# Three attention-gate column blocks computed in layer 0's first, k-outer GEMM

## The chip, the core and the metric

The kernel runs on one core of one Trainium2 chip. Engines are TensorE (PE, matmuls, with its weight loads PEld), VectorE (DVE), ScalarE (ACT), GpSimd (POOL) and SyncE (SP), which issues most DMA transfers. The metric is device time in microseconds of one execution, the median over runs.

## The reference

One inference step of a two-layer hybrid backbone on 512 latent and 128 context tokens (T = 640 columns in all), width 2048, float32. Cut to what matters:

```
mod = silu(cond) @ w_ada + b_ada                 # adaLN: shift, scale, gate (3 x 2048)
h   = rmsnorm(x) * (1 + scale) + shift
q, k, v, ag, lx, lg, hv, hx1, hx0, hg = split(h @ w_in)      # 7168 columns
att = rmsnorm(diff_attention(q, k, v)) * silu(ag)            # 8 heads, 1024 columns
lru = rglru(dwconv(lx)) * silu(lg)                           # 512 columns
hy  = hx0 * long_conv(hx1 * hv) * silu(hg)                   # 512 columns
x   = x + gate * (concat(att, lru, hy) @ w_out)
```

The column block of `ag` that belongs to head h only enters the last product of `att`, after the attention of that head.

## The kernel before

Activations lie transposed: 16 chunks of 128 features by 640 tokens. Each float32 product is made of three matmuls on split operands (wh with A high, wh with A low, wl with A high), each over two halves of 320 columns, so one 128-column block of a projection is 16 chunks times six matmuls. A weight load (`load_w`, line 369) brings up to four chunks of one block by a DMA on SP's queue into one of four `wr` buffers; ACT casts it to wh and DVE subtracts wl (lines 178, 179). The usual `gemm` (line 403) runs one column block over all 16 chunks in PSUM.

Layer 0 begins differently, because its adaLN vectors need 33 MB of w_ada before all of h exists. `run` (from line 1200) goes through five groups of chunks, (0,2), (2,2), (4,4), (8,4), (12,4). In each group it passes over the list `first`, eight column blocks (hx0 and hg, four each), with `gemm_part` (line 512): PSUM holds the sum over the group's chunks, and ACT (first group) or DVE (the others, line 527) adds it to a tile in SBUF, one of the `early` tiles. Between the blocks stand steps of `ada_piece` (line 299), each one transfer of 512 KB of w_ada and its matmuls (line 313). Two chains of steps, scale and shift, belong to each group; in all there are 10, 20, 38, 56 and 74 steps up to the end of groups 0 to 4, of which 14 come before the first block. After block number NAT (4, counted from 0) the steps that the next group needs are completed and its normalisation (`norm`) begins, one chunk after each following block, the rest behind the last block. A chunk is transposed on PE (lines 1231, 1237), scaled on DVE (line 509), cast on ACT and split on DVE.

Then `hyena_gates(0)` turns the early tiles into gates in DRAM (`md`). `layer` runs four RG-LRU blocks, the attention of eight heads, the first NAG = 3 attention gates (`gate`, line 1004, through the pool `agq`), the Hyena projections `hyena_u` with the filters, and then the Hyena convolutions beside the other five gates. A gate is a projection, a silu (`silu2`), a load of the head's attention output from `md` and of its normaliser from `rd`, two DVE products (lines 1012, 1013) and a store to `md`.

Work is ordered by a list scheduler at build time: program order is the priority, an instruction whose inputs aren't ready is passed over for a later one, weight loads are preferred, and every engine and queue then runs its own list strictly in order. So projections fill PE's gaps beside the softmax of a head.

The other adaLN pieces (layer 0's gate, layer 1's shift and scale: 12 pieces of 16 steps, 192 steps) are computed on DVE by `ada_steps` (line 320; lines 333, 335), called as a hook in `gemm` at a rate per weight load: 1 in the RG-LRU stage, 0.5 in attention, 0.75 for the first gates and the Hyena projections, 1 for the other gates and the output projection. What is left is drained near the end of `out_proj(0)`, ahead of the normalisation for layer 1.

Of the kernel before, what the change touches and what calls it, by code (L numbers as in the profile page):

```python
# [22 lines left out]
T = NL + NP  # L23
# [6 lines left out]
COL_Q, COL_K, COL_V, COL_AG = 0, 1024, 2048, 3072  # L30
COL_LX, COL_LG = 4096, 4608
COL_HV, COL_HX1, COL_HX0, COL_HG = 5120, 5632, 6144, 6656
# [4 lines left out]
WR = 4  # L37
CVB = 3
LEAD = 4
NAT = 4  # L40
MIX_ORDER = [*range(8, 12), *range(4), *range(12, 16), *range(4, 8)]


# [86 lines left out]
NAG = 3  # L130
# [7 lines left out]
class K:  # L138
# [865 lines left out]
    def gate(self, l, hs, m0, c, pool, store, bufs=1):  # L1004

        nc, V = self.nc, self.nc.vector
        sg = self.silu2(self.proj(l, m0, hs), pool, bufs=1)
        m = self.tl(pool, [128, T], tag="gm", bufs=bufs)
        nc.sync.dma_start(m, self.md[l][c])
        R = self.tl(pool, [128, T], tag="R")  # L1010
        nc.sync.dma_start(R, self.rd[l][c:c + 1, :].to_broadcast([128, T]))
        V.tensor_tensor(m, m, R, op=ALU.mult)
        V.scalar_tensor_tensor(m, m, self.par[l]["sg"], sg, op0=ALU.mult, op1=ALU.mult)
        if store or self.taps:
            nc.sync.dma_start(self.md[l][c], m)
        return m
# [183 lines left out]
    def run(self):  # L1200
        nc, tc, V = self.nc, self.tc, self.nc.vector
        dt = lambda shape, name: tc.dram_tile(shape, F32, name=name)
        self.xd = [dt([KC, 128, T], f"xd{l}") for l in range(DEPTH)]
        self.md = [dt([KC, 128, T], f"md{l}") for l in range(DEPTH)]
        self.gd = [dt([2, 5, 128, 2, 256], f"gd{l}") for l in range(DEPTH)]
        self.g1 = [dt([2, 3, 256], f"g1{l}") for l in range(DEPTH)]
        self.hd = [dt([128, 384], f"hd{l}") for l in range(DEPTH)]
        self.rd = [dt([NH, T], f"rd{l}") for l in range(DEPTH)]
        self.early = {}
        sm = self.sm  # L1210
        first = [c + j * 128 for j in range(4) for c in (COL_HX0, COL_HG)]
        w = self.i["w_in"][0]
        with ExitStack() as st, self.tc.tile_pool(name="ps0", bufs=1, space=PSUM) as self.pst:
            self.A1 = self.ctx.enter_context(self.pool("A1", 24))
# [11 lines left out]
            hs = []  # L1226
# [22 lines left out]
            def ada_to(n):  # L1249
                nonlocal done  # L1250
                while done < n:
                    next(adas, None)
                    done += 1
# [7 lines left out]
            for gi, (k0, kn) in enumerate(groups):  # L1261
                more = gi + 1 < len(groups)
                nxt = iter(())
                for n, m0 in enumerate(first):
                    self.gemm_part(self.load_w(w, k0, m0, kn), m0, hs, k0, kn, self.early[0, m0])
                    ada_to(done + (2 if kn == 4 or gi else 1))
                    next(nxt, None)
                    if more and n == NAT:
                        ada_to(steps[gi + 1])
# [9 lines left out]
                self.par.append(self.params(1, nc.sync))  # L1279
            self.sm = sm  # L1280
            self.hyena_gates(0, hs)
        self.pss = self.ctx.enter_context(self.ppool("pss", 1))
        self.pst = self.ctx.enter_context(self.ppool("pst", 2))
        self.hook = self.ada_steps([(0, p) for p in range(8, 12)] + [(1, p) for p in range(8)])
        self.layer(0, hs)
        hs = self.out_proj(0)
# [262 lines left out]
```

## Time and profile before

| what | value |
|---|---|
| median of three runs | 2725.28 us (2720.43 to 2726.11) |
| the profiled execution | 2730.49 us, of which 2728.5 us are its span |
| mean granted TensorE clock | 0.987 |
| PE busy | 2599.8 us (95%) |
| DVE busy | 1920.0 us (70%) |
| ACT, POOL busy | 1076.9 us (39%), 261.6 us (10%) |
| DMA, mean over the span | 130 GB/s |

Busy time of PE is the union of its matmuls, which overlap: a matmul of 320 columns is shown with 0.31 us, and the next one starts about 0.147 us later. The bracket behind an instruction in a timeline is the idle time of its engine before it and what ended that.

### The profile page before, as it was taken

To read this page: it belongs to the slowest core of one execution; us is meant where nothing else is said; L and a number is where in the kernel's file an instruction comes from. 1 tells how busy PE (TensorE), PEld (TensorE's weight loads), DVE (VectorE), ACT (ScalarE), POOL (GpSimd) and SP (SyncE) were. 2 spreads that over 40 slices of the span, in tenths; PEclk is the share of its full clock that TensorE was granted. 3 is DMA by queue.
4 is the path that set the end of the run, shared out by engine and by line. 5 is a ranking of instruction groups with operands and counts; after the bars stand their busy time and mean duration, and the time that the engine had idled before them with its cause. 6 is when DMAs were issued, how large, how long until landed. Compare 5 with 4: busy or idle time off the path is not lost. (4 is left out here: it accounts for less than half of the span.)

```text
span 2728.5 us, 45802 instructions
## 1 busy us (share of the span) xinstructions
PE 2599.8 (95%) x17503; PEld 2485.5 (91%) x17503; DVE 1920.0 (70%) x3499; ACT 1076.9 (39%) x1970; POOL 261.6 (10%) x352
## 2 busy tenths in 40 slices
PE   4999989999999999989998999999999999999998
PEld 2589989999999998889998999999999999989997
DVE  3568997787888787777679467877777756564333
ACT  4224545455554222132235256444455522223222
POOL 1000220000000221200001012000000021120000
PEclk9999999999999999999999999999999999999999
DMA  8773443332333545576664323422322252345333
GB/s 256 247 239 118 128 136 90 90 106 66 102 93 114 173 136 158 158 227 200 191 196 147 117 69 86 127 87 86 101 75 64 59 166 79 106 143 158 98 94 118
DMA packets 439911, 354.83 MB, mean 130 GB/s; under 512 B 26746, under 2 KB 367618, under 8 KB 439436
## 3 DMA queue, kind: packets, MB, share of 16 engines
q1 hardware_dynamic: 428618, 336.39, 41.1%
q10 hardware_dynamic: 9586, 9.42, 1.1%
q0 software_dynamic: 1488, 6.10, 0.6%
q8 instruction: 137, 2.24, 0.3%
q14 instruction: 82, 0.67, 0.1%
HBM read 316.51 MB, written 35.32 MB: 129 GB/s over the span
## 5 line engine op out<-in xcount | busy, mean ns | idle before, releaser
L420 PE MATMUL g<-A,wh 128*128 128x320 f32 x8320 | 1614.1, 311 | 5.6 <-ACT A L178 5.0
L420 PEld LDWEIGHTS g<-A,wh 128*128 128x128 f32 x8320 | 1321.3, 189 | 7.3 <-ACT A L178 5.3
L420 PE MATMUL g<-A,wl 128*128 128x320 f32 x4160 | 963.9, 310 | 0.0
L178 ACT CAST wh<-wr 128x512 fp32r<-128x512 f32 (+1 forms) x592 | 362.1, 613 | 966.3 <-PE g L420 696.2
L420 PEld LDWEIGHTS g<-A,wl 128*128 128x128 f32 x4160 | 702.6, 189 | 0.2
L179 DVE TENSOR_TENSOR wl<-wr,wh 128x512 fp32r<-128x512 f32 (+1 forms) x592 | 429.2, 728 | 339.0 <-ACT wh L178 323.9
L335 DVE SCALAR_TENSOR_TENSOR adas<-wa,cs,adas 128x512 f32<-128x512 f32 x480 | 363.9, 784 | 61.4 <-DMA wa<-in_w_ada 60.1
L1160 ACT ACTIVATE e<-e,mx 128x768 f32<-128x768 f32 (+1 forms) x160 | 133.7, 835 | 69.2 <-DVE e L1159 68.9
L1159 DVE TENSOR_SCALAR_CACHE_REDUCE e<-pS 128x768 f32<-128x768 f32 (+1 forms) x160 | 131.0, 819 | 9.1 <-PE pS L713 3.9
L1122 POOL TENSOR_TENSOR oq<-ot 128x640 f32<-128x640 f32 x16 | 20.9, 1309 | 912.5 <-ACT ot L1118 689.7
L713 PE MATMUL pS<-kk,qq 128*128 128x384 f32 (+1 forms) x288 | 100.3, 348 | 3.9 <-DVE e L1159 3.4
L521 PE MATMUL gp<-A,wh 128*128 128x320 f32 x512 | 101.9, 318 | 1.0 <-ACT wh L178 1.0
L397 PE MATMUL g<-A,wh 128*128 128x320 f32 (+2 forms) x384 | 92.9, 324 | 8.9 <-DVE A L492 5.9
L521 PEld LDWEIGHTS gp<-A,wh 128*128 128x128 f32 x512 | 79.7, 189 | 23.0 <-issue 11.2
L713 PE MATMUL pS<-kl,qq 128*128 128x384 f32 (+1 forms) x288 | 95.2, 331 | 0.0
L179 DVE TENSOR_TENSOR wtl<-pt,wth 128x512 fp32r<-128x512 f32 (+1 forms) x144 | 70.1, 522 | 29.6 <-ACT wth L178 29.3
L178 ACT CAST wth<-pt 128x512 fp32r<-128x512 f32 (+1 forms) x144 | 59.7, 459 | 61.6 <-PE pt L1103 60.0
L313 PE MATMUL pa<-wada,csw 128*32 128x512 f32 (+1 forms) x320 | 52.7, 565 | 28.9 <-DVE st L436 21.5
L397 PEld LDWEIGHTS g<-A,wh 128*128 128x128 f32 x384 | 67.0, 194 | 14.4 <-DVE A L492 8.3
L1396 DVE SCALAR_TENSOR_TENSOR xf<-g,mod,xo 128x128 f32<-128x128 f32 (+3 forms) x96 | 38.3, 432 | 55.8 <-PE g L420 23.2
L1166 DVE SCALAR_TENSOR_TENSOR e<-e,rz,e 128x768 f32<-128x768 f32 (+1 forms) x80 | 70.6, 882 | 1.7
L713 PEld LDWEIGHTS pS<-kk,qq 128*128 128x128 f32 x288 | 54.0, 187 | 14.7 <-DVE e L1159 8.8
(353 smaller groups left out, 3159.7 us busy)
## 6 DMA issues: line engine op xcount, KB each, us to landing
wr<-in_w_in SPq DMA_DIRECT2D x440, 256.0 KB
wa<-in_w_ada SPq DMA_DIRECT2D x256, 256.0 KB
wada<-in_w_ada SPq DMA_DIRECT2D x64, 512.0 KB
wr<-in_w_out SPq DMA_DIRECT2D x128, 256.0 KB
mx<-md SPq DMA_DIRECT2D x28, 320.0 KB
md<-ot SPq DMA_DIRECT2D x16, 320.0 KB
gm<-md SPq DMA_DIRECT2D x16, 320.0 KB
R<-rd SPq DMA_DIRECT2D x16, 320.0 KB
```

The source lines that it names most:

```text
L178: self.nc.scalar.copy(hi, src)
L179: self.nc.vector.tensor_tensor(lo, src, hi.bitcast(F32), op=ALU.subtract)
L313: nc.tensor.matmul(acc[32 * q:32 * q + 32, :], lhsT=self.csw[:, k, :], rhs=w[:, j, :], start=k < 4, stop=k >= 12, tile_position=(0, 32 * q))
L335: nc.vector.scalar_tensor_tensor(acc[:, s], w, c, acc[:, s], op0=ALU.mult, op1=ALU.add)
L397: nc.tensor.matmul(p[:, j, o:o + c1 - c0], lhsT=w[:, c, :], rhs=rhs[k][x][:, c0:c1], start=(a == 0 and c == 0 and n == 0), stop=(a == 3 an ...
L420: nc.tensor.matmul(p[:, j, :HT], lhsT=w[:, c, :], rhs=rhs[k][x][:, j * HT:(j + 1) * HT], start=(a == 0 and c == 0 and n == 0), stop=(a == ...
L521: nc.tensor.matmul(p[:, j, :HT], lhsT=w[:, c, :], rhs=rhs[k0 + c][x][:, j * HT:(j + 1) * HT], start=(c == 0 and t == 0), stop=(c == n - 1 ...
L713: self.nc.tensor.matmul(out, lhsT=a, rhs=b, start=(n == 0), stop=(n == len(pairs) - 1))
L1159: V.tensor_scalar(e[:, :nk].rearrange("p (a b) -> p a b", a=nhf), ps[:, :nhf, :hw], -1.0, None, op0=ALU.mult, op1=ALU.min, accum_out=mx)
L1160: nc.scalar.activation(e[:, :nk], e[:, :nk], AF.Exp, scale=-1.0, bias=mx, accum_out=Z[:, c:c + 1])
L1166: V.scalar_tensor_tensor(es[0][:, :nk], es[1][:, :nk], rz[:, 1:2], es[0][:, :nk], op0=ALU.mult, op1=ALU.add)
L1396: V.scalar_tensor_tensor(x[:, a:b], p, mod[:, 32 + m, s:s + 1], xo[:, a:b], op0=ALU.mult, op1=ALU.add)
```

## The change

Three more column blocks, the attention gates of heads 0 to 2, join the list `first`, so each of the five groups passes over 11 blocks, and there are 11 early tiles. After `hyena_gates(0)` their silu is taken and stored to a new DRAM tensor `agd`. In layer 0, `gate` loads this for heads 0 to 2 in place of its own projection and silu; with that the hook is not called there. NAT goes from 4 to 8. Layer 1 is as before.

```diff
-NAT = 4
+NAT = 8
@@ gate
-        sg = self.silu2(self.proj(l, m0, hs), pool, bufs=1)
+        if l == 0 and c < NAG:
+            sg = self.tl(pool, [128, T], tag="th")
+            nc.sync.dma_start(sg, self.agd[c])
+        else:
+            sg = self.silu2(self.proj(l, m0, hs), pool, bufs=1)
@@ run
+        self.agd = dt([NAG, 128, T], "agd")
-        first = [c + j * 128 for j in range(4) for c in (COL_HX0, COL_HG)]
+        first = [c + j * 128 for j in range(4) for c in (COL_HX0, COL_HG)] + [COL_AG + h * 128 for h in range(NAG)]
@@ run, behind the first GEMM
             self.hyena_gates(0, hs)
+            with self.pool("ag0") as ap:
+                for h in range(NAG):
+                    th = self.silu2(self.proj(0, COL_AG + h * 128, hs), ap)
+                    nc.sync.dma_start(self.agd[h], th)
```

## Rows read from the trace of the kernel before

**Rows 1.** The page, parts 1 and 2: engines' busy time; DMA by 40 slices.
```profile
PE 2599.8 (95%) x17503; PEld 2485.5 (91%) x17503; DVE 1920.0 (70%) x3499; ACT 1076.9 (39%) x1970; POOL 261.6 (10%) x352
...
DMA  8773443332333545576664323422322252345333
```

**Rows 2.** Waits of PE over the span: total us, times, longest us.
```profile
PE pa L313 <- DVE st L436: 21.5, 1, 21.5
...
PE pa L313 <- DMA wada<-in_w_ada: 7.4, 5, 3.3
...
PE g L397 <- DVE A L492: 5.9, 9, 1.2
```

**Rows 3.** Stretches of the first GEMM: length, busy us, clock, DMA share, GB/s.
```profile
40.00:60.00 20.00, 17.71 (x131) 10.79 (x127) 9.93 (x45) 6.77 (x16) 0.00 (x0) 0.83 0.94 289
...
140.00:160.00 20.00, 20.00 (x136) 14.31 (x135) 11.45 (x21) 5.63 (x9) 0.00 (x0) 1.00 0.98 311
...
50.00:120.00 70.00, 65.93 (x395) 40.31 (x395) 38.41 (x89) 22.55 (x44) 1.50 (x9) 0.98 0.82 250
```

**Rows 4.** PE's timeline around its wait for w_ada: start, us, instruction, idle before.
```profile
87.00 1.06 PE L313 MATMUL pa<-wada,csw 128*32 128x512 f32 x8
...
95.36 1.58 PE L313 MATMUL pa<-wada,csw 128*32 128x512 f32 x4 [3.26 <-DMA wada<-in_w_ada]
96.87 1.43 PE L521 MATMUL gp<-A,wh 128*128 128x320 f32 x4
98.23 1.50 PE L313 MATMUL pa<-wada,csw 128*32 128x512 f32 x4
99.66 0.56 PE L521 MATMUL gp<-A,wl 128*128 128x320 f32 x2
```

**Rows 5.** PE's timeline in the last group of the first GEMM.
```profile
201.08 1.35 PE L521 MATMUL gp<-A,wh 128*128 128x320 f32 x7
...
207.56 0.75 PE L521 MATMUL gp<-A,wh 128*128 128x320 f32 x4
208.14 0.45 PE L521 MATMUL gp<-A,wl 128*128 128x320 f32 x2
208.44 0.75 PE L521 MATMUL gp<-A,wh 128*128 128x320 f32 x4
```

**Rows 6.** DVE's groups from 180 to 230 us: busy us, mean ns, idle before.
```profile
L527 DVE TENSOR_TENSOR e<-e,gp 128x640 f32<-128x640 f32 x13 | 10.7, 819 | 3.1 <-PE gp L521 2.9
L179 DVE TENSOR_TENSOR wl<-wr,wh 128x512 fp32r<-128x512 f32 x13 | 8.9, 685 | 0.0
...
L509 DVE TENSOR_SCALAR hn<-pn,mod 128x512 f32<-128x512 f32 x4 | 3.2, 802 | 0.0
```

**Rows 7.** Stretches around attention's end, the first gates and the Hyena projections.
```profile
843.00:868.00 25.00, 25.00 (x175) 24.78 (x174) 24.36 (x51) 14.87 (x31) 0.00 (x0) 1.00 0.36 108
868.00:905.00 37.00, 35.27 (x231) 33.99 (x231) 32.11 (x50) 14.33 (x28) 6.38 (x10) 0.95 0.51 157
```

**Rows 8.** Timelines of DVE, POOL and PE around attention's end.
```profile
872.22 0.88 DVE L1013 SCALAR_TENSOR_TENSOR gm<-gm,sg,th 128x640 f32<-128x640 f32 x1
...
898.20 0.82 DVE L439 TENSOR_TENSOR oh<-oh,ol 128x640 f32<-128x640 f32 x1
...
893.18 0.16 POOL L746 MEMSET cv<- 128x1 f32 x3
...
883.29 0.56 PE L713 MATMUL pt<-ol,onesr 128*128 128x320 f32 x2 [1.73 <-POOL ol L1124]
```

**Rows 9.** The stretch of the RG-LRU stage's later part.
```profile
300.00:420.00 120.00, 104.58 (x665) 102.55 (x664) 113.59 (x163) 56.96 (x80) 26.68 (x21) 0.93 0.45 131
```

**Rows 10.** The hook's DVE operations from 843 us on; DVE and stretch at the layer border.
```profile
L335 DVE SCALAR_TENSOR_TENSOR adas<-wa,cs,adas 128x512 f32<-128x512 f32 x67 | 52.0, 799 | 6.2 <-DMA wa<-in_w_ada 6.0
...
1400.67 1.29 DVE L342 TENSOR_REDUCE mod<-pt 128x4 f32<-128x512 f32 x2 [2.90 <-PE pt L341]
...
1440.00:1460.00 20.00, 15.69 (x89) 12.89 (x88) 20.00 (x39) 14.53 (x33) 7.56 (x7) 1.00 0.54 162
```

## The prediction

> **What bounds the kernel now.** I read the busy shares first: TensorE (PE) is busy 95% of the span and no other engine comes near [rows 1]. Then I asked what PE waits for [rows 2]: the largest wait, 21.5 us, is before its first matmul and the change leaves it alone. What remains is scattered. So 42 us of PE work that only moves from one full stretch to another is worth nothing in itself; the change can win only idle time that the moved work fills, and lose only idle time that it makes. The reader should therefore look at the two places: where the work goes (the first GEMM, about 50 to 228 us) and where it leaves (the attention gates after layer 0's attention, about 843 to 905 us).
>
> **Where it goes.** The slices show the DMA engines 70 to 80% busy in the first 200 us [rows 1], which looks like a transfer-bound stage with room on PE. By stretches it is not so: from 50 to 120 us PE is busy 65.93 of 70 us [rows 3], and PE's only wait on a w_ada piece after the GEMM has begun is 3.26 us at 95.36 [rows 4]. Behind that stall the clock fell to its lower level (1.2 GHz): three bundles at 95.36, 96.87 and 98.23 stand 1.51, 1.36 and 1.43 us apart (to 99.66), where they take about 1.0, 0.7 and 1.0 at 2.4 GHz, so 1.6 us more. Stall and slow clock are 3.3 + 1.6 = 4.9 us: this is all the idle time that the moved work can fill here.
>
> **The moved work.** In the last k group, where no adaLN piece is in between, four wh and two wl matmuls (one k chunk of one column block) take 208.44 - 207.56 = 0.88 us [rows 5]. A block has 16 chunks: 14.1 us; three blocks: 42.2 us. They are added to the first GEMM and taken from the gates, with the same shapes. There PE is busy 25.00 of 25 us and 35.27 of 37 [rows 7], so the blocks fill their place after attention: minus 42.2 us there.
>
> **Is the stall gone?** By the code each group runs its blocks with adaLN steps between (512 KB of w_ada each, 0.524 MB). Before, groups 0 and 1 take 16 block loads of 0.131 MB and steps 14 to 44: 2.1 + 15.7 = 17.8 MB. Their PE work is 16 x 1.76 us, some 27 us of steps (1.06 us each from the four-chunk groups on [rows 4], half of it before) and about 8 us of transposes and filter matmuls: 64 us, so 280 GB/s are asked. After, 22 loads and steps 14 to 47 are 20.2 MB against 39 + 30 + 8 = 77 us: 262 GB/s. The queue delivered 289 in 40 to 60 us and 311 in 140 to 160, at a share of 0.98 [rows 3]. NAT = 8 also takes away the burst: before, five steps stand in a row behind the fifth block of group 1; after, two follow every block. I take the 4.9 us as won; the bounds are 0 and 4.9.
>
> The Trainium skill (DMA: Bandwidth & Descriptors, Specifications) gives a core about 358 GB/s from HBM; by that figure the stall would go with a wide margin, and the sum is the same. The 311 GB/s at a share of 0.98 say that here little more is to be had.
>
> **What is late next in the first GEMM.** With NAT = 8 of 11 blocks the next group's chunks come after blocks 9 and 10, so three of four chunk transposes stand behind the last block instead of two. Each needs two DVE operations (802 ns the larger [rows 6]), an ACT cast and a DVE subtraction before PE may read the chunk. Before, PE bridged this by interleaving two blocks (the bundle of seven wh matmuls at 201.08 [rows 5]) without a gap. One chunk more is at worst 1.7 us (two chunks of work, 1.76 us, against some 3.5 us) at each of four group borders: 0 to 6.8 us. Three of the borders have adaLN steps to fill with, so I take 1. DVE gets 12 additions of 0.82 us, 15 splits (nine of 0.69, six of half width, say 0.4), and three silu products of about 0.8: 21 us in a stretch that grows by 37 us; it isn't the bound. The three stores to agd are behind the hyena gates on SP and nothing on PE waits for them.
>
> **Where it leaves.** Gates 0 to 2 become three loads, two DVE products (0.88 us the second [rows 8]) and a store each. Their inputs exist long before attention ends, so they lie beside it; in SP's queue the loads stand ahead of weight loads, but four weight buffers are 4 x 3.5 = 14 us ahead. What now fills PE's gaps beside head 7's softmax is no longer an attention gate but the first Hyena projections. Their eviction needs three `cv` buffers in memory that attention held. The zeroing of `cv` at 893.18 had no wait of its own [rows 8], but it stood behind other POOL work; so they are free by 893 and perhaps much sooner. I charge 1 us; bounds 0 and the price of rival 3. The existing stalls there (1.73 us at 883.29 [rows 8]) belong to attention's end and stay.
>
> **The adaLN hook.** A step is two DVE operations of about 0.8 us [rows 10] and a w_ada load. The gates' 12 chances at rate 0.75 made nine steps; these now fall later. Layer 0 offers 197 steps for 192 before, 188 after; four are left for the drain inside the output projection. Before, the last scale piece ended at 1400.67 and the next piece began at once [rows 10]; after, the last one ends some 30 us later relative to its surroundings, still ahead of chunks 12 to 15 of the norm that want it. DVE is full there (20.00 of 20 us [rows 10]) but gets no more steps than before, only others. I take 0; bounds -2 and 13.4 us (nine steps of 1.49).
>
> **Sum.** -42.2 (gates) + 42.2 (first GEMM) - 4.9 (stall) + 1 (chunk borders) + 1 (Hyena start) + 0 (hook) = -2.9 us. The profiled execution took 2730.49 us (2728.5 of span), 5.2 above the median; set against the median: 2725.3 - 2.9 = **2722.4 us**, 0.1% less. A measurement can tell about 0.2%, 5.5 us, from no change.
>
> **Rivals.**
> 1. *It does not do what it says.* Transfers still come late once the blocks are longer, or the late chunks eat what the stall gave: 0 to +2 us, 2725 to 2727. Against it are 262 against 280 GB/s asked; for it is that PE's order is fixed and a piece in the wrong place stalls it with other work ready, as at 95.36. Chance 0.2, all within 0.2%.
> 2. *More than the stall goes.* From 300 to 420 us the LRU stage is held by DVE: 113.59 us of 120 busy, PE only 104.58 [rows 9]. If the longer first GEMM takes over DVE work that now lies ahead of this stage (the last eight operations of the first adaLN piece, 6 us), and the stall after attention changes place too (1.7 us and its slow clock, another 1.7), then 4.9 + 6 + 3.4 = 14 us at most; I price it at 9 us: 2716. Against it: before 300 us DVE has idle time, so what it is relieved of earlier should not reach the LRU stage. Chance 0.28.
> 3. *Slower: the Hyena projections cannot be evicted beside attention.* Two blocks fill both PSUM buffers at about 885 us; if `cv` or the buffers behind it are tied to attention's last operation (0.82 us from 898.20 [rows 8]), the third block waits from 885 to 899 on PE and a slow clock follows: 14 + 1.7 - 1 = 15 us, 2737. It decides where eviction is later than 885. A wait of half that gives 2730. For it: DVE is 24.36 of 25 us busy just there [rows 7], and POOL's memsets stand in one queue. Against it: `cv` waited on nothing at 893. Chance 0.12.
> 4. *Slower: the nine late steps reach the layer border.* Half of the 13.4 us appears as PE waits on the norm's DVE operations, of which 5.9 us exist already [rows 2]: +7, 2729 or more. Chance 0.08.
>
> **How the numbers follow.** The forecast itself has 0.32. Faster by over 0.2% (below 2719.8): rival 2 and the forecast's lower edge, 0.3. Slower by over 0.2% (above 2730.7): rivals 3 and 4 nearly whole, 0.18. Within: 0.52. The range takes rival 2 without its far end and half of rival 3: 2713 to 2733.
>
> The Trainium skill (TensorE: Matmul & The Clock Gate, What's actually happening) says that an idle PE array falls to 1.2 GHz and comes back after work. The 1.6 us behind the stall agree; if a rival makes a stall of its own, as much again is to be added, which rival 3 does by the row.
>
> **What would show it.** Right: no PE wait on w_ada beyond 0.5 us after the GEMM has begun; the first GEMM longer by 37 to 39 us; gates 0 to 2 done before head 7; the stretch from the last V projection of head 7 to the last Hyena projection shorter by about 42 us. Wrong: a new PE wait of several us around 105 to 130 us or at group borders, a PE gap where the first Hyena PSUM is evicted, more than 8 us of waits of the layer-1 norm's matmuls, or a LRU stage of another length.

## The result, and the profile after

The changed kernel takes 2755.85 us (median of four runs, 2753.88 to 2764.36) against 2725.70 for the kernel before, measured beside it: ratio 1.0121, 95% interval 1.0103 to 1.0139, some 30 us slower. The forecast was 2722.4, in a range of 2713 to 2733. The profiled execution of the changed kernel took 2754.26 us, 2752.3 of it span.

Because the forecast leaned on one profiled execution of the kernel before, that kernel was profiled once more (2727.37 us, span 2725.3). The two tables below cut both executions at the same events: the first GEMM; layer 0's RG-LRU stage; the first seven heads of layer 0's attention; three parts of what I call *the Hyena stretch* (from head 7's first transposes to the first Hyena transposes, on to the last ones, on to the first transposes of the output projection); and last the layer border with layer 1's gates and RG-LRU stage, up to its first head. Columns: stretch, its length, busy us of PE, PE's weight loads, DVE, ACT and POOL (instructions in brackets), granted clock, DMA share, GB/s. The kernel before, second execution:

```profile
50.86:225.62 174.76, 171.98 (x1108) 129.94 (x1108) 114.37 (x222) 52.76 (x95) 1.83 (x15) 1.00 0.74 232
225.62:407.57 181.95, 166.72 (x1089) 163.86 (x1089) 163.11 (x259) 89.00 (x128) 36.89 (x37) 0.96 0.43 126
407.57:825.51 417.94, 412.26 (x2798) 399.51 (x2799) 334.04 (x656) 215.47 (x417) 22.20 (x14) 1.00 0.31 91
825.51:941.51 116.00, 113.32 (x768) 110.88 (x766) 97.67 (x160) 45.20 (x85) 20.18 (x33) 1.00 0.51 155
941.51:1063.56 122.05, 112.80 (x767) 109.96 (x767) 96.58 (x167) 27.09 (x59) 17.68 (x34) 0.99 0.42 120
1063.56:1184.24 120.68, 108.06 (x739) 103.01 (x740) 94.76 (x164) 24.66 (x40) 24.25 (x27) 0.97 0.61 189
...
1391.47:1715.74 324.27, 311.34 (x2073) 303.42 (x2071) 226.40 (x383) 147.43 (x249) 51.48 (x63) 0.99 0.39 115
```

The changed kernel:

```profile
48.22:265.49 217.27, 216.36 (x1398) 172.71 (x1399) 145.58 (x292) 65.31 (x120) 2.00 (x18) 1.00 0.68 212
265.49:446.75 181.26, 165.34 (x1088) 162.99 (x1087) 152.42 (x219) 87.94 (x124) 36.65 (x34) 0.96 0.41 121
446.75:867.18 420.43, 414.01 (x2799) 401.33 (x2800) 338.66 (x660) 215.44 (x417) 22.44 (x14) 0.99 0.33 97
867.18:972.82 105.64, 78.96 (x515) 75.15 (x512) 81.54 (x142) 35.94 (x71) 21.74 (x33) 0.90 0.42 126
972.82:1085.03 112.21, 105.62 (x711) 103.30 (x711) 87.47 (x149) 25.52 (x56) 15.21 (x34) 0.97 0.38 112
1085.03:1199.65 114.62, 106.30 (x744) 101.34 (x744) 89.39 (x156) 25.94 (x41) 23.82 (x27) 1.00 0.60 186
...
1406.94:1739.61 332.67, 315.22 (x2073) 304.28 (x2071) 246.14 (x407) 146.24 (x248) 53.31 (x63) 0.99 0.40 120
```

Read row against row: the first GEMM +42.5 us; attention +2.5; the Hyena stretch 358.73 to 332.47, -26.3; layer border to layer 1's first head +8.4. The rest (start, layer 0's RG-LRU stage, output projection, the rest of layer 1) sums to -0.1. Together +27.0, the difference of the spans 2752.3 and 2725.3. So the work arrived at its full price and left at less than two thirds of it, although eleven steps of the adaLN hook left the Hyena stretch together with it (table of experiment 9).

Where it did not leave, the list of PE's waits shows one new entry (total us, times, longest), and the timelines of the changed kernel show its chain. Columns: start, length, engine, line, operation, out<-in; in brackets the engine's idle time before it and what ended it; ACTq, SPq are the engines' queues issuing transfers.

```profile
PE g L420 <- ACT cv L749: 20.0, 2, 19.4
...
948.53 1.44 PE L420 MATMUL g<-A,wh 128*128 128x320 f32 x4 [19.39 <-ACT cv L749]
```

```profile
928.89 0.62 ACT L178 CAST wh<-wr 128x512 fp32r<-128x512 f32 x1 [2.90 <-PE g L420]
933.25 0.37 ACTq L580 DMA_DIRECT2D hid<-hd  x1
940.82 1.22 ACTq L587 DMA_DIRECT2D w<-in_hy_w  x2
942.68 0.23 ACTq L603 DMA_DIRECT2D drow<-in_hy_d  x1
946.30 1.31 ACTq L605 DMA_DIRECT2D dec<-in_decay  x3
947.65 0.43 ACT L747 COPY cv<-g 128x320 f32<-128x320 f32 x1 [18.15 <-DVE adas L335]
```

```profile
921.43 0.58 POOL L733 DMA_DIRECT2D tb<-in_dft  x1
...
937.17 1.95 POOL L586 MEMSET w<- 64x1024 f32 x2 [14.08 <-DVE oh L435]
```

```profile
922.06 0.33 SPq L329 DMA_DIRECT2D wa<-in_w_ada  x1
...
937.69 0.97 SPq L373 DMA_DIRECT2D wr<-in_w_in  x2
```

```profile
932.30 0.75 DVE L335 SCALAR_TENSOR_TENSOR adas<-wa,cs,adas 128x512 f32<-128x512 f32 x1 [8.15 <-DMA wa<-in_w_ada]
932.97 4.15 DVE L435 RECIPROCAL oh<-oq 128x640 f32<-128x640 f32 x1
...
942.03 0.82 DVE L439 TENSOR_TENSOR oh<-oh,ol 128x640 f32<-128x640 f32 x1
```

From the bottom up: an adaLN step waits 8.15 us for its transfer. SP issued this at 922.06, 0.6 us behind the first and largest of the three loads of transform tables (921.43; 2.1 of 2.7 MB in all); that table landed at 931.85 and the transfer at 932.21. DVE works its queue in order, so attention's last reciprocal and its Newton steps stand behind it. The filters' loads go into memory that attention holds until these are done, and are issued from ACT's queue, where they stand ahead of the copies (line 747) that empty the two PSUM buffers. PE has filled both and stops for 19.39 us. In the kernel before, the gates' blocks ran on PE in this time, with buffers of their own to be evicted into: the three gates were PE's *cover* [rows 7, 8].

### The profile page after: what moved, and what is told of

Its sections match the earlier page's. It is cut to its first block, busy times and chain, and to the rows that moved or that the text cites. A ratio compares the mean times of both kernels' runs of the same rounds, so it can differ in the third digit from the quotient of the medians.

```text
span 2752.3 us, 45818 instructions
## 1 busy us (share of the span) xinstructions
PE 2600.9 (94%) x17503; PEld 2483.2 (90%) x17503; DVE 1933.3 (70%) x3514; ACT 1078.8 (39%) x1976; POOL 261.5 (10%) x352
## 5 line engine op out<-in xcount | busy, mean ns | idle before, releaser
L420 PE MATMUL g<-A,wh 128*128 128x320 f32 x8128 | 1576.1, 311 | 22.9 <-ACT cv L749 20.0
L420 PEld LDWEIGHTS g<-A,wh 128*128 128x128 f32 x8128 | 1289.8, 189 | 25.2 <-ACT cv L749 20.5
L420 PE MATMUL g<-A,wl 128*128 128x320 f32 x4064 | 943.4, 311 | 0.0
L420 PEld LDWEIGHTS g<-A,wl 128*128 128x128 f32 x4064 | 686.3, 189 | 0.2
L521 PE MATMUL gp<-A,wh 128*128 128x320 f32 x704 | 139.4, 316 | 1.6 <-ACT wh L178 1.0
L521 PEld LDWEIGHTS gp<-A,wh 128*128 128x128 f32 x704 | 109.3, 188 | 28.9 <-issue 10.1
L521 PE MATMUL gp<-A,wl 128*128 128x320 f32 x352 | 81.5, 310 | 0.0
L397 PEld LDWEIGHTS g<-A,wh 128*128 128x128 f32 x384 | 64.6, 188 | 18.1 <-DVE A L500 6.5
```

Of the source, the lines that this page charges most:

```text
L397: nc.tensor.matmul(p[:, j, o:o + c1 - c0], lhsT=w[:, c, :], rhs=rhs[k][x][:, c0:c1], start=(a == 0 and c == 0 and n == 0), stop=(a == 3 an ...
L420: nc.tensor.matmul(p[:, j, :HT], lhsT=w[:, c, :], rhs=rhs[k][x][:, j * HT:(j + 1) * HT], start=(a == 0 and c == 0 and n == 0), stop=(a == ...
L521: nc.tensor.matmul(p[:, j, :HT], lhsT=w[:, c, :], rhs=rhs[k0 + c][x][:, j * HT:(j + 1) * HT], start=(c == 0 and t == 0), stop=(c == n - 1 ...
```

## The experiments

The diffs are cut to the lines that matter.

**1. Was the stall at 95.36 the kernel's?** The kernel before, unchanged, profiled again.

> The kernel before, unchanged, profiled once more. In the kernel whose gates do not advance the hook, which has the same program in the first GEMM, that GEMM took 173.6 us (first to last of its matmuls) and not 176.8, without a wait of 3.26 us and a slow clock. Theory that the stall at 95.36 belonged to the one profiled execution: 173 to 175 us here, no wait on w_ada above 2 us behind 60 us. Rival, the stall belongs to the kernel: 176 to 177.5 us and a wait of about 3 us near 95.

The first GEMM took 174.76 us, and the largest wait on w_ada after 50 us was this (total, times, longest):

```profile
PE pa L313 <- DMA wada<-in_w_ada: 2.8, 2, 1.5
```

Four other kernels with the same program in this stage took 175.17, 174.17, 173.70 and 171.95 us, with 1.9, 2.2, 1.8 and 0 us of waits on w_ada; the profile that the prediction read, 177.4. So the 3.26 us and the slow clock behind them [rows 4] belonged to one execution, and a wait of some 2 us belongs to the kernel.

**2. NAT.** The changed kernel with one number put back.

```diff
-NAT = 8
+NAT = 4
```

> Changed kernel with NAT back at 4, so the adaLN steps of the next group stand in one burst behind the fifth of eleven blocks. The prediction counted NAT = 8 as what takes the wait on w_ada away. If so, the first GEMM (217.3 us in the changed kernel) grows by 3 us or more, with waits on w_ada of several us. Rival: eleven blocks ask for less transfer in any case, and with the chunks' normalisation begun earlier the group borders are better covered: 217 us or less, no wait on w_ada above 2 us.

216.24 us for the first GEMM and no wait on w_ada in it; ratio to before 1.0121 (1.0098 to 1.0145), the same as with 8. So the rival holds: eleven blocks take the burst with either value, and the spread over nine blocks shows no gain.

**3. Only the half that leaves.**

```diff
-        sg = self.silu2(self.proj(l, m0, hs), pool, bufs=1)
+        if l == 0 and c < NAG:
+            sg = self.tl(pool, [128, T], tag="th")
+            nc.sync.dma_start(sg, self.md[l][12 + c])
+        else: ...
```

> Only one half of the change: the gates of heads 0 to 2 are loaded in layer 0 (a Hyena gate is read in their place) and their projections are left out altogether; list, NAT and first GEMM as in the kernel before. So 42.2 us of PE work are taken away and nothing is added. If they are worth only what the stages of the changed kernel gave back (-26.2 from head 7 to the output projection, +8.4 at the border and in layer 1's RG-LRU stage, +2.5 in attention), the span is 2725.3 - 15.3, about 2710, and PE's wait at the first Hyena eviction is 17 us or more. If the loss in the changed kernel has to do with the longer first GEMM (other order, other memory), the span is near 2725.3 - 42.2 + 8, about 2691, with a wait of 6 us or less there.

This kernel leaves the three projections out and so does not compute the result; only its time counts. Ratio 0.9959 (0.9946 to 0.9972): 42.2 us of PE work taken away, nothing added to the first GEMM, and the kernel gets 11 us shorter. The three parts of its Hyena stretch sum to 336.43 us, with a wait of 16.64 us at the first Hyena eviction:

```profile
826.29:932.53 106.24, 83.99 (x515) 80.00 (x512) 81.53 (x141) 35.37 (x71) 21.72 (x33) 0.87 0.42 126
932.53:1044.73 112.20, 105.73 (x714) 103.26 (x711) 86.30 (x149) 26.10 (x57) 15.80 (x34) 0.97 0.38 112
1044.73:1162.72 117.99, 106.53 (x744) 101.31 (x744) 89.78 (x156) 25.95 (x41) 23.85 (x27) 1.00 0.59 181
```

So the loss is there without the longer first GEMM. That the wait is a little under, and the span (2715.2) a little over, what was expected changes nothing in this. The kernel with the three gates and without their hook steps (experiment 8) stands at 1.0016; it has as many hook steps in the Hyena stretch (48). Between the two the 42.2 us are worth 0.57%, some 15.5 us of the medians, give or take 5.

**4. The links of the chain, one at a time.** Filters from the second pair of projections on; tables behind the filters' hidden layer; both; tables in five parts.

```diff
-                self.filt, self.fs = self.filters(l, fp, nc.scalar), 4
+                    if j == (1 if l == 0 else 0):
+                        self.filt = self.filters(l, fp, nc.scalar)
```

> Changed kernel, but in layer 0 the generator of the Hyena filters starts with the second pair of projections instead of the first, so that on ACT's queue the eviction copies of the first Hyena projection stand ahead of the filters' loads. Queue theory: PE's wait of 19.4 us at 948.5 comes from evictions standing behind loads that wait for attention's memory; it falls to 6 us or less, the clock keeps its upper level for most of the stretch, and the profiled run gets 13 to 18 us shorter than the changed kernel's (2754 to some 2738). Rival, memory theory: the eviction buffers themselves come free only with attention's last DVE operations (about 939 us); then the wait stays at 10 us or more and the gain is under 9 us.

```diff
         q.dma_start(hid, self.hd[l])
+        if l == 0:
+            self.fill_tabs(hid)      # the three table loads, behind hid
```

> Changed kernel, but layer 0's transform tables (2.7 MB) are asked for only after the filters' hidden layer has been loaded, so that they no longer run in front of the adaLN transfer for which DVE waits 8.15 us at 932.30. Theory that the tables start the chain: that wait falls below 2 us, the reciprocal behind it starts near 925 instead of 932.97, the filters' loads and the evictions come about 8 us earlier, PE's wait is 11 to 12 us, and the run gets 7 to 10 us shorter (2754 to some 2746). Rival: the filters' loads wait for something else in attention's end, and the tables only happened to be there; then PE's wait stays at 17 us or more and the gain is under 3 us.

> Changed kernel with both edits: the filters start with the second pair of projections, and the tables are asked for behind the filters' hidden layer. Theory of two obstacles in a row, each hiding the other (late evictions behind the filters' loads; the hook transfer and the weights behind the tables): PE waits 7 us or less in all between 925 and 965 us, the stretch from head 7 to the output projection falls from 539.8 to 525 or less, the run to some 2738. Rival, without the gates' cover the 2.7 MB of tables collide with whatever transfer stands there: a wait of 7 us or more for weights, a hook transfer or a filter load remains, the stretch is 533 or more, the run 2746 or more.

> As the last one, but the tables come in five parts, each asked for only after one filter block has been computed, so that no more than 0.5 MB of them stands in front of another transfer. If the collision with the tables is what is left, PE's waits between 925 and 1000 us fall to 6 us or less, the stretch from head 7 to the output projection is 524 or less and the run some 2737. Rival, it is the missing cover itself (attention's last DVE and ACT work holds what the first Hyena blocks need, whatever the tables do): the stretch stays at 533 or more.

Each link went where it was aimed at and the time did not follow: ratios 1.0146 (1.0128 to 1.0164), 1.0130 (1.0114 to 1.0145), 1.0113 (1.0095 to 1.0130) and 1.0127 (1.0104 to 1.0149). Filters later: the first eviction comes at 931.16, so its buffers were free and the rival that blamed their memory falls; but PE then waits 13.61 us for the first transposes, and the filters that start later are left over at the end (last part of the stretch 132.72 us instead of 114.62). Tables late: the reciprocal starts at 926.68, as expected, and the tables, now issued at 937.22, hold up the next transfer instead, a filter load. With both edits, and with the tables in parts, head 7 to the end of the output projection takes 542.49 and 545.46 us, as both rivals have it (533 or more). PE's waits with the filters later; then, with the tables late, PE's waits and what DVE waits for before the second (the first is for a load issued at 934.50, ahead of the tables; the second comes from one issued at 940.21, behind them):

```profile
958.97 1.09 PE L775 MATMUL pt<-ident,uS 128*128 128x128 f32 x4 [13.61 <-DVE uS L771]
```

```profile
938.20 3.75 PE L615 MATMUL pt<-w,hid 128*128 128x256 f32 x8 [7.94 <-DMA w<-in_hy_w]
950.03 2.08 PE L615 MATMUL pt<-w,hid 128*128 128x256 f32 x4 [8.08 <-DVE sx L617]
...
949.28 0.69 DVE L617 TENSOR_TENSOR sx<-pt,dec 128x512 f32<-128x512 f32 x1 [7.59 <-DMA dec<-in_decay]
```

The Hyena stretch stays at 336.38, 330.41, 333.63 and 336.17 us.

**5. The hook out of attention's end.** Off during head 7 and the first pair, alone; with filters from the second pair at five steps a block; and with the tables late as well.

```diff
+                    if l == 0 and h == NH - 1:
+                        self.hr = 0
                     fin = self.attention(l, hs, h, kl, pool, fin)
```

> Changed kernel, but in layer 0 the hook is not advanced during head 7 and the first pair of Hyena projections, so that no adaLN step stands in front of attention's last DVE operations (the reciprocal waited 8.15 us behind one). Theory that the in-order hook step starts the chain: the reciprocal starts near 926 instead of 932.97, PE's first wait at a Hyena eviction falls from 19.4 to 12 us or less, and idle time of PE from head 7 to the end of the Hyena stage (41.6 us in the changed kernel, 17.3 in the kernel before without gate hook) falls by 7 or more. Rival, as with the late tables the wait is only handed on to the next transfer or issue in line: 17 us or more of waits remain between 925 and 965. The postponed steps cost about as much later, so the whole time may not fall by more than 5 us in either case.

> As the last one, and the filters start with the second pair of projections at five steps for each block instead of four, so that as many are done by the end of the projections as before (starting later at four left filters behind them, uncovered). Theory of separate obstacles (hook step, filters' loads ahead of evictions, filters left over at the end): idle time of PE from head 7 to the end of the Hyena stage 25 us or less instead of 41.6, the run 2740 or less. Rival, without the gates there is not enough other work beside the end of attention and the beginning of the filters: 35 us or more of idle time there, the run 2748 or more.

> As the last one, with the tables asked for behind the filters' hidden layer as well. If the 2.7 MB of tables still delay a transfer that someone waits for, this run has 4 us or more less idle time of PE between head 7 and the end of the Hyena stage than the last one (25 us or less in all); if they only collide with the next transfer, as when they alone came later, it has the same or up to 8 us more.

This is the head of the chain. With the hook off alone the reciprocal starts at 919.18 and PE waits 4.14 us instead of 19.39:

```profile
933.71 1.44 PE L420 MATMUL g<-A,wh 128*128 128x320 f32 x4 [4.14 <-ACT cv L749]
```

With all three, PE is busy 70.84 of 73.92 us up to the first Hyena transposes. PE's idle time in the whole stretch is 25.80, 30.71 and 27.90 us instead of 41.6: in the first kernel it falls as expected, in the other two it lies between theory and rival. But the stretch only falls to 324.29, 321.98 and 318.45 us, while 14 hook steps have left it, and these cost more later: from the layer border to layer 1's first head these kernels take 350.40, 350.94 and 350.51 us instead of 332.67. Ratios 1.0162, 1.0142 and 1.0130. My theory of separate obstacles at one place was true of the place and false of the time.

**6. Two early gates, one kept as cover.**

```diff
+NEAR = 2   # in the list, in agd and in gate's condition, instead of NAG
```

> Changed kernel with two early gates instead of three: the third gate's projection (14.1 us of PE) stays behind layer 0's attention and is evicted into its own memory. Theory that the gates were the cover for the end of attention: PE's wait for the first Hyena eviction falls from 19.4 us to 6 us or less, the stretch from head 7 to the output projection's last matmuls is no more than 537 us (539.8 with three early gates, 558.0 with none early and no hook steps in the gates; 529.9 would be without any loss), the first GEMM is some 14 us shorter than in the changed kernel, and the run comes out near 2735 to 2740. Rival, the wait is made by an order that does not depend on the cover: 17 us or more of wait, the stretch 550 or more, the run near 2752.

The wait at the first Hyena eviction is 6.46 us, close to the 6 us of the cover theory. But head 7 to the end of the output projection takes 548.02 us, between the theories (537 and 550); the Hyena stretch is 338.98 us, only 7.6 less than 332.47 + 14.1; and the run is no faster (1.0128, 1.0110 to 1.0146). Its first GEMM is 210.12 us, 7.2 shorter instead of 14, with 3.4 us of idle time and a clock of 0.99. That NAT = 8 leaves one of ten blocks behind the burst may be why; no run shows it.

**7. Three other gates.** Those of heads 3 to 5, from beside the convolutions; heads 0 to 2 as before.

```diff
-        if l == 0 and c < NAG:
+        if l == 0 and NAG <= c < 2 * NAG:
```

> Changed kernel with the same number of early gates, but those of heads 3 to 5, which else run beside the Hyena convolutions; the gates of heads 0 to 2 stay behind attention, projected as in the kernel before, and the loaded gates still advance hook and convolutions. Theory that the moved gates were the cover of attention's end: the stretch from head 7 to the first Hyena transposes takes 115 to 119 us with 4 us or less of idle time, as in the kernel before (116.0 to 117.8), and not 26.7 us of idle time; the 42 us come out of the convolutions' stretch, less what is uncovered there. If nothing is uncovered there the span is 2725 + 42.5 - 42.2 + 2, about 2728. Rival, the moved work is cover wherever it stood: the convolutions' stretch gives back 15 us or more, the run is 2745 or more.

Both halves of this come out as the cover theories say. The first two of the three parts of the Hyena stretch are as in the kernel before; the last, out of which 42.2 us of PE work were taken, is as long as before:

```profile
867.36:983.24 115.88, 113.33 (x769) 110.87 (x766) 97.41 (x160) 45.33 (x85) 20.07 (x33) 1.00 0.51 155
983.24:1102.89 119.65, 111.43 (x766) 108.40 (x767) 96.41 (x167) 27.10 (x59) 17.69 (x34) 1.00 0.42 123
1102.89:1222.66 119.77, 75.24 (x439) 66.12 (x439) 96.07 (x169) 14.88 (x24) 22.84 (x27) 0.76 0.59 183
```

PE idles 44.5 of 119.77 us, its clock is granted at 0.76 (below 1 the lower level, 1.2 GHz, for part of the time), and the length doesn't move: 120.68 before. Ratio 1.0162 (1.0134 to 1.0189). DVE is busy as long as before (96.07 against 94.76; eight hook steps more fell into this part, in place of the DVE work that left with the gates), and waits another 9.5 us for the hook's transfers. So what this part shows is the loss of 42.2 us of PE work together with a gain of eight steps.

**8. The nine late hook steps, alone and put back.** In the kernel before, no hook in the three gates; in the changed kernel, the hook advanced in the three loaded gates.

```diff
-            self.hr = rate["ag1"]
+            self.hr = rate["ag1"] if l else 0
```

> Kernel before, only that the hook is not advanced in layer 0's first three attention gates (nine steps fall later); gates, first GEMM and everything else as before. Theory that the late steps alone cost layer 1: its gates and RG-LRU stage is 251 us or more instead of 243.5 and the run is 7 to 11 us longer than the kernel before (2730 to some 2739). Rival: 243 to 246 us there and less than 3 us in all. Nothing is expected at the Hyena start.

> Changed kernel, but the three loaded gates still advance the hook (nine steps), as the three computed gates did before. Theory that the late steps cost layer 1: its gates and RG-LRU stage, 243.5 us before and 253.7 in the changed kernel (from the layer border to layer 1's first attention head), goes back to 245 or less, and the run gets 7 to 11 us shorter (2754 to some 2745), if the Hyena start keeps its wait of about 19 us. Rival: the stage is longer for another reason (another order of its work); then it stays at 252 or more and the time changes by less than 3 us, or grows by up to 5 because the nine steps add DVE work before attention's last operations.

The place is right, the price is not. From the layer border to layer 1's first head: 334.02 us without the gates' hook in the kernel before (324.27 with), 324.15 with it in the changed kernel (332.67 without). But what the late steps cost there, they had cost in the Hyena stretch: 348.61 against 358.73, and 346.32 against 332.47. In all the first kernel is at 1.0016 of before (1.0003 to 1.0029), the second at 1.0132 (1.0111 to 1.0154) where the changed kernel stands at 1.0121.

**9. What the removal is worth when DVE has little to do.** Experiment 8 had shown DVE steps to cost time in a stretch that I had taken as PE's. So the hook was taken out of the whole Hyena stretch in both kernels (in head 7 as in experiment 5, and in the first three gates).

```diff
-                self.hr = rate["hv"]
+                self.hr = rate["hv"] if l else 0
-                    self.hr = rate["ag2"]
+                    self.hr = rate["ag2"] if l else 0
```

> Changed kernel with the adaLN hook off in layer 0 from head 7 to the end of the Hyena convolutions (those steps are made up in the output projection, which gets long; only the stretch from head 7 to the first transposes of the output projection is of interest, 332.5 us in the changed kernel with 48 hook steps in it). If DVE's work, of which the hook is a third here, is what keeps the 42.2 us from being gained, the stretch is 291 to 308 us and 34 to 42 us shorter than that of the kernel before with the same edit. If it is the chain of waits at the Hyena start and in the filters, whatever DVE has to do, it is 318 us or more and at most 25 us shorter than the other.

> Kernel before with the hook off in the same stretch (358.7 us there with 59 hook steps, of which PE is busy 334). Both theories: 334 to 348 us, PE the bound. It is the measure for the run beside it: the difference of the two stretches is what 42.2 us of PE work taken out are worth when DVE has little to do.

The changed kernel without hook, then the kernel before without hook, in the three parts of the Hyena stretch:

```profile
870.28:961.23 90.95, 81.06 (x507) 75.97 (x504) 59.35 (x105) 35.40 (x71) 21.86 (x33) 0.94 0.33 101
961.23:1068.62 107.39, 101.89 (x704) 99.67 (x704) 64.41 (x113) 25.57 (x57) 14.65 (x34) 1.00 0.27 78
1068.62:1184.41 115.79, 109.76 (x758) 105.60 (x758) 70.17 (x121) 28.88 (x46) 22.45 (x27) 0.99 0.51 159
```

```profile
822.40:938.77 116.37, 113.27 (x761) 109.93 (x758) 73.48 (x124) 44.95 (x85) 18.02 (x33) 1.00 0.39 119
938.77:1049.37 110.60, 106.72 (x738) 104.63 (x738) 66.39 (x114) 26.34 (x58) 14.19 (x34) 1.00 0.28 81
1049.37:1165.09 115.72, 108.24 (x757) 103.99 (x757) 68.82 (x121) 27.56 (x45) 22.71 (x27) 1.00 0.51 158
```

The length of the whole Hyena stretch, by the hook steps in it (operations of lines 333 and 335, two for a step):

| hook steps in the stretch | gates projected there | gates loaded | difference, of 42.2 us of PE work |
|---|---|---|---|
| 59 | 358.73 (before) | 346.32 (experiment 8) | 12.4 |
| 48 | 348.61 (experiment 8) | 332.47 (changed) | 16.1 |
| 0 | 342.69 | 314.13 | 28.6 |

Each length is of one execution. How far these go apart is seen in others: the first profile of the kernel before has 356.79 us where the second has 358.73, and two more kernels with 48 steps and the gates gone have 334.96 (experiment 2) and 336.43 (experiment 3) where the changed kernel has 332.47. So 12.4 and 16.1 are not told apart, and 28.6 stands clear of both.

The result lies between the two theories (34 to 42, and at most 25). Both are at work: of the 26.1 us that the changed kernel lacks by this table, 12.5 come back when the hook is gone, and 13.6 don't. Of these, 6.8 are idle time up to the first Hyena transposes (9.89 against 3.10 us), and at most 5.5 are what a clock of 0.94 over 90.95 us comes to; the remainder I can't place. The same columns say what a step costs: 48 steps lengthen the stretch by 5.9 us while the gates are there and by 18.3 without them.

Two things this pair of runs does not separate. With a hook step not only its DVE work leaves, but also its transfer of 0.26 MB and DVE's waits for that at the head of its queue (15.9 us of waits in the changed kernel's Hyena stretch, beside 258.4 us of work). And every edit lets the scheduler order the stretch anew.

**10. DVE relieved by POOL.** From the second pair on, the weights' low parts on POOL, in both kernels.

```diff
-        self.split(wh, wl, wr)
+        nc.scalar.copy(wh, wr)
+        nc.gpsimd.tensor_tensor(wl, wr, wh.bitcast(F32), op=ALU.subtract)
```

> Changed kernel, but from layer 0's second pair of Hyena projections to the end of its convolutions the low parts of the weights (wl, 44 subtractions of some 0.69 us) are computed on POOL instead of DVE; PE's work and the order of the program stay. Over the kernels so far the length from head 7 to the first transposes of the output projection follows DVE's work there (332.5 us at 258.4 of DVE in the changed kernel, 358.7 at 289.0 before, 348.6 at 275.7 without gate hook, 355.3 at 289.9 with 42 us of PE work taken out of the convolutions). Theory that DVE's work sets this length: 30 us less of it makes the stretch 15 to 26 us shorter (307 to 317) and the run some 2732. Rival, the length is a chain of single operations and transfers, which less DVE work elsewhere does not shorten: 328 us or more, the run within 5 us of the changed kernel, or slower because POOL takes longer for each.

> The same edit in the kernel before. There PE has 334 us of work in the 358.7 us of the stretch, so that by the DVE theory PE is the next bound: 8 to 16 us shorter (343 to 351), the run some 2712. By the rival within 5 us of the kernel before, or slower.

Both became slower, 1.0214 (1.0197 to 1.0232) and 1.0080 (1.0065 to 1.0095), with stretches of 363.34 and 383.47 us. That is as the rival has it: a subtraction takes 1526 ns on POOL. It settles nothing about DVE, since DVE wasn't relieved: in the kernel before its busy time there falls from 289.0 to 282.6 us instead of by 30, because its other operations took longer. Two-input operations of DVE from the second pair to the convolutions, in the changed kernel and with the subtractions on POOL (count, busy us, mean ns, idle before):

```profile
L833 DVE TENSOR_TENSOR yf<-yy,yy 128x512 f32<-128x512 f32 x8 | 5.5, 684 | 1.9 <-POOL yy L804 1.9
L801 DVE TENSOR_TENSOR y<-pt,yy 128x512 f32<-128x512 f32 (+1 forms) x10 | 6.8, 682 | 2.5 <-DMA yy<-gd 1.7 <-POOL rr L847 0.8
L769 DVE TENSOR_TENSOR uS<-cv 128x256 f32<-128x256 f32 x3 | 1.2, 412 | 0.0
```

```profile
L838 DVE TENSOR_TENSOR yf<-yy,yy 128x512 f32<-128x512 f32 x8 | 8.6, 1079 | 3.8 <-POOL yy L809 3.8
L806 DVE TENSOR_TENSOR y<-pt,yy 128x512 f32<-128x512 f32 (+1 forms) x10 | 6.8, 683 | 9.6 <-DMA yy<-gd 8.2 <-issue 0.8 <-PE pt L718 0.6
L774 DVE TENSOR_TENSOR uS<-cv 128x256 f32<-128x256 f32 x4 | 4.8, 1210 | 4.8 <-POOL cv L769 4.8
```

No kernel that does the whole work beat the one before, and on these numbers none of this kind can by much: in its first GEMM PE idles 174.76 - 171.98 = 2.8 us (0.1 in the run of experiment 9), which is all that moved work could fill there.

## Why the prediction was wrong

**The stall (-4.9): mis-sized, from one execution.** Its mechanism was read rightly, and the wait is gone (PE is busy 216.36 of 217.27 us). But it was worth some 2 us (2.8 us of idle time before, 0.9 after; waits on w_ada of 0 to 2.8 us in five executions with eight blocks, experiment 1), not 4.9; the profiled execution was the one 5.2 us above the median, which the prediction noted and did not use.

**The moved work in the first GEMM (+42.2, and +1 at the borders): right.** 217.27 - 174.76 = 42.5, where the prediction's own sign, with the stall won, said 37 to 39; PE's busy time there grew by 44.4 and its idle time fell by 1.9. The 2.2 us above 42.2 may be chunk borders; no run separates them.

**The gates (-42.2): the step that failed.** The argument was that PE is busy 25.00 of 25 and 35.27 of 37 us there [rows 7], so PE's work is the length. A full PE shows only that the scheduler found something to put on it. In the same row DVE is busy 24.36 of 25, and the blocks stood beside attention's last steps and the filters' loads. Taken out at the same number of hook steps they are worth 16.1 us in the table of experiment 9 and some 15.5 by the medians of experiments 3 and 8; taken out with no hook step left there, 28.6. Taken out of the convolutions, with eight steps more beside them, they are worth nothing that shows in that part's length (experiment 7). So the loss has two parts that the runs show, the chain of waits at attention's end and the hook's steps; whether a step costs by DVE's work, by its transfer or by the wait for that stays open.

**The Hyena start (+1): wrong by some 18 us of waiting.** Rival 3 named the place, the third projection that cannot be evicted, and 15 us for it; the wait is 19.4. Its cause was another: not `cv` in attention's memory (the eviction at 931.16 in experiment 4), but an adaLN step at the head of DVE's queue and the filters' loads at the head of ACT's (experiments 4 and 5). The prediction listed what the moved steps issue, but not the loads of the stage *behind* the gates, which now came 42 us closer to attention's end.

**The hook (0): right as a sum, for a reason that wasn't given.** The late steps cost 8 to 10 us, near rival 4's price, but not where it said. The border itself got shorter; layer 1's RG-LRU stage, where they now run, got longer. The two parts in the second execution of the kernel before, then in the changed kernel:

```profile
1391.47:1472.07 80.60, 68.86 (x428) 62.47 (x427) 70.62 (x151) 40.81 (x91) 16.43 (x20) 0.98 0.53 153
1472.07:1715.74 243.67, 242.48 (x1648) 240.95 (x1646) 155.78 (x233) 106.62 (x160) 35.04 (x43) 1.00 0.35 102
```

```profile
1406.94:1485.90 78.96, 68.90 (x423) 60.58 (x422) 72.09 (x155) 39.21 (x87) 17.40 (x20) 1.00 0.53 157
1485.90:1739.61 253.71, 246.32 (x1652) 243.70 (x1650) 174.05 (x253) 107.03 (x161) 35.91 (x43) 0.99 0.36 109
```

DVE's work in the second part grows from 155.78 to 174.05 us, and the part by 10.0. The same steps save 10 to 14 us in the Hyena stretch (experiment 8), where the forecast had them as free.

**The gates' products beside attention (0): 2.5 us.** Six DVE products lie beside the heads now; DVE is busy 338.66 instead of 334.04 us and the heads take 420.43 instead of 417.94. With heads 0 to 2 left alone it is 417.64.

**Rival 2 (-9): it failed as the prediction's own argument against it had it.** The longer first GEMM did take DVE work out of layer 0's RG-LRU stage (163.11 to 152.42 us), but the stage stayed as long (181.95, 181.26). The work came out of its first 74 us, where PE is busy 74.38 of 74.38 us in the kernel before (second execution, DVE 60.69 there and 50.26 in the changed kernel); in the 120 us behind, DVE has 113.48 and 113.61.

**The range and the chances.** Slower by over 0.2% had a chance of 0.18, and no rival had the size: 3 and 4 together come to 15 + 7 us. Every number that kept the forecast near zero took a stage that PE fills as a stage that PE sets. With 16.1 instead of 42.2 for the gates (the wait at the Hyena start is in this), 2 instead of 4.9 for the stall and 2.5 for attention, the same sum gives 42.2 + 1 - 2 - 16.1 + 2.5 = +27.6; that is a reckoning after the fact, on the executions that it is set against (+27.0).

## What to carry to other kernels

Before you count an engine's removed work as time, ask what the other engines do in the same stretch: if a second one has much to do, or a serial tail lies beside it, the removed work was its cover and only part of it comes back. Price the stage that moves up into the freed place as you price the change: which transfers it issues, on whose queue, and into whose memory. And take a stall that you mean to win from at least two executions.

## What the runs showed of the hardware

DVE operations with both inputs in SBUF became longer where POOL subtracted: 412 to 1210 ns and 684 to 1079 ns in the mean of the rows of experiment 10, while the one with an input in PSUM stayed at 682 and 683. The means mix two kinds. In the changed kernel with the subtractions on POOL, the operations of line 774 that began during a subtraction took 1466 to 1480 ns, and those of line 838 took 1680 to 1774; those of line 838 that began outside one stayed at 671 to 693. The Trainium skill (SBUF — State Buffer, Who interferes with whom) says that DVE and GpSimd share a pair of ports and that a DVE instruction with two SBUF inputs contends with a GpSimd instruction that reads SBUF; the trace agrees.

In the changed kernel a 0.26 MB load that SP issued at 922.06, 0.6 us behind a 2.1 MB load issued by POOL, landed after 10.2 us, at 932.21. With the tables asked for later, the same load was issued at 923.17 and landed after 2.8 us, at 925.92; the tables delayed a filter load instead. The Trainium skill (DMA: Bandwidth & Descriptors, Issuing engines are not separate DMA queues) says that transfers of different issuers share the same 16 engines; the two runs agree.
